# Layer 0's opening in a two-layer backbone: row blocks loaded first, LayerNorm applied on ACT, transposes per row block, and half of three column tiles computed early

## The chip, the cores and the metric

The kernel runs on one core of a Trainium2 chip. The metric is the device time of one launch in microseconds (us). The median of three runs of the kernel before is 1859.11 us.

## The reference, cut to what matters

A two-layer transformer-like backbone over 256 context tokens and 256 latent tokens, each of width 1024. At the start of a layer the tokens are normalised and modulated with vectors that come from a conditioning vector through a large matrix (adaLN); the result is projected by `w_in`, whose first columns feed the Hyena branch:

```python
s_lat, s_ctx = silu(c), silu(c_ctx)
mod   = s_lat @ ada_w[i] + ada_b[i]          # and mod_c from s_ctx
sh1, sc1, g1, sh2, sc2, g2 = split(mod, 6)
u  = layer_norm(h)  * (1 + sc1)  + sh1       # latent rows
uc = layer_norm(hc) * (1 + csc1) + csh1      # context rows
p_hy, p_sw, p_rw, p_df, p_gt = split(u @ w_in[i])
kf = rfft(filter made by a small MLP with sine activations)   # Hyena filter
y_hy = x2 * longconv(x1 * longconv(v, kf0), kf1)              # v, x1, x2: depthwise conv of p_hy
...                                          # three more branches, merge, output projection, FFN
```

## The kernel before, in words

**Tiling.** Tokens are held as four row blocks of 128 rows x 1024: `xn[0..3]` (two of context, two of latent tokens). After the norm they are transposed on TensorE into eight blocks of 128 channels x 512 tokens, one block for each k. A float32 product is done as three float32r matmuls: each operand is split into a rounded high part and a low remainder. `uh[k]`, `ul[k]` are the two parts of the modulated tokens; `whi`, `wlo` those of a 128x1024 weight tile, made by `wcut` (L193: ACT casts to `whi`, L197, then DVE or POOL subtracts into `wlo`, L201). One output column tile (128 output channels x 512 tokens) is `dense` (L243): for each of the eight k three matmuls of 512 columns into a PSUM bank, 24 in all. The first six column tiles of layer 0 are Hyena's (`hyena_cols`, L627); behind each a depthwise convolution (`conv3`, L321) of one ACT and two DVE instructions empties the bank.

**Modulation vectors.** `ada` (L362) computes them in groups of four 512 KB tiles of `ada_w`; each tile has two matmuls against a 32-column stationary tile. Then comes a tail: ACT copies the bank (L382), TensorE transposes it, DVE reduces it and adds the bias (L388, L390), and for scale groups adds one (L394). Group 0 is the shift for k = 0 to 3, group 2 the scale for k = 0 to 3, groups 1 and 3 the same for k = 4 to 7. `modulate` (L461) transposes two row blocks at a time and then, for each k, ACT makes `uh` (L475), POOL an intermediate (L476) and DVE `ul` (L478).

**Norm.** `stats` (L416) is two bn_stats, an aggregate and an add on DVE and a power on POOL; `norm` (L446) applies mean and scale, in the opening as one DVE instruction over 128x1024 (L451).

**Filter MLP.** `filter_mlp` (L497) loads four small tensors and does two steps, each one or two small matmuls, eight DVE instructions (L516, then `sin_rr`) and a Sin on ACT (L495). `filters` (L520) then makes each filter's spectrum: four matmuls with `fw3` (L531), DVE products, absolute values on ACT and sums on POOL for a norm `hyn` that the convolutions of column tiles 2 to 5 need, and eight products with the DFT matrix (L574).

**Order around the change.** `lockstep` (L279) writes instructions in a fixed order for PE, DVE, ACT and POOL: it draws from `start()` (L1786) and, by the credits that `start()` yields, from `ada`. Loads go on SP's queue in the order in which they are written; a load whose buffer is still in use waits, and all loads behind it wait too. In the opening `ada` takes its tiles from the buffers `w`, `whi`, `wlo` (seven in all, L375). Behind the fixed order `weave` (L267) mixes `hyena_cols` with `filters`, with a ratio of 0.7 that says how much filter work is written for each unit of dense work; there the framework's scheduler may move an instruction forward where it expects an engine to be free. `col_tile` (L257) also draws two steps of layer 0's remaining `ada` groups for each column tile (`N.rate`, `N.side`). PSUM has eight banks: three of tag `d`, four of tag `m`, one of tag `o`.

## Time and profile before

| | us |
|---|---|
| median of three runs | 1859.11 (1858.53 to 1861.16) |
| the profiled execution, whole | 1862.13 |
| its span from first to last instruction | 1860.1 |
| PE busy | 1702.9 (92%) |
| DVE busy | 1145.5 (62%) |
| ACT busy | 787.3 (42%) |
| POOL busy | 641.4 (34%) |
| span before the first Hyena column tile has been half computed | 55.35 |
| convolution of the sixth Hyena column tile starts | 107.41 |

A busy share of PE says that matmuls were in flight, not that they ran at the full clock; the views by stretch give the granted clock beside it. Idle time of an engine counts only where PE, which carries most of the chain that ended last, waits for it.

### The profile page before, as it was taken

The numbers are of one execution on the slowest core, as the hardware profiler recorded it, in microseconds if no ns is written. First come the engines' busy times: TensorE is split into PE (matmuls) and PEld (weight loads), VectorE is DVE, ScalarE is ACT, GpSimd is POOL, SyncE is SP. The second block draws the span as 40 slices with busy tenths as digits, with TensorE's granted clock in tenths as the row PEclk, the third lists the DMA queues.
The fourth block names the chain that finished last, engine by engine and source line by source line (L and its number), as shares of the span: only waits on it lengthen the run. The fifth ranks groups of instructions, "written<-read, shape, count | busy, mean of one in ns | idle before, by whom it ended". The sixth has DMA issues, their size and how long they took to land.

```text
span 1860.1 us, 36364 instructions
## 1 busy us (share of the span) xinstructions
PE 1702.9 (92%) x14618; PEld 1354.4 (73%) x14618; DVE 1145.5 (62%) x2204; ACT 787.3 (42%) x1579; POOL 641.4 (34%) x782
## 2 busy tenths in 40 slices
PE   6999999998999988999999998899788998879987
PEld 2566778776777766877787776677687887679964
DVE  5566456775665478544555657563765665758887
ACT  2323345653232346433334444334553343356632
POOL 2313144544544126101010164244454664131153
PEclk9999999999999999999999999999889999889999
DMA  8353321211111455344334556653123222646543
GB/s 302 126 198 113 130 69 57 83 57 45 45 56 55 148 196 189 120 150 139 125 102 138 180 175 210 198 179 130 47 88 97 88 65 82 237 142 189 184 145 113
DMA packets 73456, 241.37 MB, mean 130 GB/s; under 512 B 8518, under 2 KB 17096, under 8 KB 73032
## 3 DMA queue, kind: packets, MB, share of 16 engines
q1 hardware_dynamic: 69336, 229.80, 37.6%
q10 hardware_dynamic: 3952, 9.25, 1.5%
q8 instruction: 115, 1.88, 0.4%
q14 instruction: 53, 0.43, 0.1%
HBM read 235.84 MB, written 2.13 MB: 128 GB/s over the span
## 4 chain that ended last, share of the span: by engine, by line
PE 60%; DVE 15%; ACT 5%; DMA 4%; POOL 3%; issue 3%; POOLq 0%; SPq 0%; ACTq 0%; DVEq 0%
PE bkd L174 45%; PE bkm L174 8%; PE bkm L1362 2%; PE bko L174 2%; DVE wlo L201 2%; PE bkm L178 2%; ACT whi L197 2%; DMA w<-in_wdn 1%; DMA w<-in_wout 1%; DMA w<-in_win 1%; DVE sV L1340 1%; DVE dmx L978 1%; ACT dp L981 1%; POOL wlo L201 1%; DMA w<-in_adaw 1%
## 5 line engine op out<-in xcount | busy, mean ns | idle before, releaser
L174 PE MATMUL bkd<-uh,whi 128*128 128x256 f32 (+1 forms) x1624 | 585.7, 361 | 7.1 <-ACT whi L197 3.3
L174 PE MATMUL bkd<-uh,wlo 128*128 128x256 f32 (+1 forms) x1624 | 555.4, 342 | 3.5 <-DVE wlo L201 3.2
L174 PE MATMUL bkd<-ul,whi 128*128 128x256 f32 (+1 forms) x1624 | 552.9, 340 | 0.0
L197 ACT CAST whi<-w 128x256 fp32r<-128x256 f32 (+1 forms) x532 | 333.7, 661 | 268.4 <-PE bkd L174 116.6
L201 DVE TENSOR_TENSOR wlo<-w,whi 128x1024 fp32r<-128x1024 f32 (+3 forms) x247 | 284.2, 1155 | 195.7 <-ACT whi L197 194.8
L201 POOL TENSOR_TENSOR wlo<-w,whi 128x256 fp32r<-128x256 f32 (+2 forms) x328 | 276.9, 863 | 314.2 <-ACT whi L197 307.6
L174 PEld LDWEIGHTS bkd<-uh,whi 128*128 128x128 f32 x1624 | 311.8, 192 | 85.1 <-ACT whi L197 24.0
L174 PEld LDWEIGHTS bkd<-uh,wlo 128*128 128x128 f32 x1624 | 311.7, 192 | 40.8 <-DVE wlo L201 3.8
L174 PEld LDWEIGHTS bkd<-ul,whi 128*128 128x128 f32 x1624 | 312.9, 193 | 26.6 <-issue 0.7
L1722 POOL TENSOR_TENSOR fc<-fc,fc 128x256 f32<-128x256 f32 (+1 forms) x47 | 46.2, 982 | 331.3 <-DVE fc L329 312.0
L174 PE MATMUL bkd<-w,sst 128*32 128x512 f32 x348 | 81.0, 646 | 18.3 <-DMA w<-in_adaw 18.2
L1584 POOL TENSOR_TENSOR acc<-acc,tg 128x512 f32<-128x512 f32 (+1 forms) x32 | 32.5, 1017 | 145.4 <-DVE tg L1583 132.4
L324 ACT ACTIVATE fc<-bkd,vec 128x256 f32<-128x256 f32 (+1 forms) x94 | 60.8, 647 | 7.5 <-PE bkd L174 7.5
L327 DVE SCALAR_TENSOR_TENSOR fc<-bkd,vec,fc 128x255 f32<-128x255 f32 (+1 forms) x94 | 54.8, 583 | 11.5 <-ACT fc L324 11.5
L174 PE MATMUL bkd<-wlo,hh 128*128 128x512 f32 x126 | 52.4, 416 | 9.3 <-DVE wlo L201 6.2
L237 ACT CAST hh<-fc 128x256 fp32r<-128x256 f32 (+1 forms) x47 | 23.2, 493 | 84.9 <-POOL fc L1722 84.9
L329 DVE SCALAR_TENSOR_TENSOR fc<-bkd,vec,fc 128x255 f32<-128x255 f32 (+1 forms) x94 | 55.3, 589 | 2.9
L238 DVE TENSOR_TENSOR hl<-fc,hh 128x256 fp32r<-128x256 f32 (+1 forms) x47 | 25.6, 545 | 47.4 <-ACT hh L237 47.4
L174 PE MATMUL bkd<-y,wbh 128*128 128x512 f32 (+1 forms) x192 | 54.6, 369 | 0.0
L238 DVE TENSOR_TENSOR wbl<-wb,wbh 128x256 fp32r<-128x256 f32 x48 | 29.3, 611 | 37.0 <-ACT wbh L237 36.7
L174 PE MATMUL bkd<-whi,hh 128*128 128x512 f32 x126 | 48.5, 399 | 3.7 <-DVE fc L329 2.3
L981 ACT ACTIVATE dp<-bkm,dmx 128x512 f32<-128x512 f32 (+1 forms) x48 | 29.6, 617 | 48.2 <-DVE dmx L979 40.2
(474 smaller groups left out, 2995.6 us busy)
## 6 DMA issues: line engine op xcount, KB each, us to landing
w<-in_adaw SPq DMA_DIRECT2D x87, 512.0 KB, 3.9
w<-in_wup SPq DMA_DIRECT2D x82, 512.0 KB, 3.5
w<-in_wdn SPq DMA_DIRECT2D x66, 512.0 KB, 3.5
w<-in_wg SPq DMA_DIRECT2D x64, 512.0 KB, 3.5
w<-in_win SPq DMA_DIRECT2D x58, 512.0 KB, 3.6
w<-in_wout SPq DMA_DIRECT2D x24, 512.0 KB, 3.6
wb<-in_wbr SPq DMA_DIRECT2D x48, 128.0 KB, 3.4
pw<-in_wup SPq DMA_DIRECT2D x8, 512.0 KB, 4.5
```

Source lines behind the costliest of these rows:

```text
L174: self.nc.tensor.matmul(out, lhsT, rhs, start=start, stop=stop)
L178: self.nc.tensor.transpose(out, in_, self.ident[0:n, 0:n])
L197: self.nc.scalar.copy(hi[:, c], w[:, c])
L201: e.tensor_tensor(lo[:, c], w[:, c], hi[:, c].bitcast(F32), ALU.subtract)
L238: nc.vector.tensor_tensor(lo, src, hi.bitcast(F32), ALU.subtract)
L324: nc.scalar.activation(dst, ps, AF.Identity, bias=b, scale=w1)
L327: nc.vector.scalar_tensor_tensor(d3[:, :, 1:256], p3[:, :, 0:255], w0, d3[:, :, 1:256], ALU.mult, ALU.add)
L329: nc.vector.scalar_tensor_tensor(d3[:, :, 0:255], p3[:, :, 1:256], w2, d3[:, :, 0:255], ALU.mult, ALU.add)
L981: nc.scalar.activation(p[:, 0:n], ps[:, 0:n], AF.Exp, scale=scale, bias=mx[:, hc], accum_out=zz[:, hc])
L1362: nc.tensor.matmul(ps[r, o:o + 32], L(r, d, c, x, e, j), R[r, d, 2 * e + j, :], start=True, stop=True, tile_position=(r.start, r.start))
L1584: nc.gpsimd.tensor_tensor(acc, acc, tg[:, 0:n], ALU.add)
L1722: nc.gpsimd.tensor_tensor(ab[0], ab[0], ab[1], ALU.mult)
```

## The change

`start()` is written anew and `ada` is drawn by hand within it. The four row blocks are loaded first, with the small MLP tensors between them; the layer's `row` tensor moves from ACT's queue to SP's. The norm is applied on ACT. Transposes go by row block: `turned` takes four k of one row block as soon as that block is normalised, and holds all four `m` banks; `modulated` then works for each k on both halves of the tokens. `ada` gets nine buffers of its own and the bank of tag `o`; the MLP uses bank `d`. Three Hyena column tiles get the first half of their sum (k = 0 to 3) inside the fixed order (`begin`); the second half is taken up by `col_tile`. The first weight tile's low part is made on POOL. No filter step is in the opening any more, and the weave ratio is 1.5 in layer 0. Column tiles that were begun early do not draw steps of the remaining `ada` groups.

```diff
-    def dense(self, ps, hi, lo, c0, xh, xl, nk, t0, t1):
-        for k in range(nk):
+    def dense(self, ps, hi, lo, c0, xh, xl, nk, t0, t1, ks=None):
+        for k in ks or range(nk):
...
     def col_tile(self, src, part):
+        if self.begun:
+            rest_, ps = self.begun.pop(0)
+            yield from rest_
+            return ps
         hi, lo = self.wsplit(src)
...
-        nc.scalar.dma_start(self.row[l], a["row"][l].partition_broadcast(128))
+        (nc.scalar if l else nc.sync).dma_start(self.row[l], a["row"][l].partition_broadcast(128))
...
-            ps = self.bank("d")
+            ps = self.bank("o" if early else "d")
...
-                tag = ("w", "whi", "wlo", "w", "whi", "w", "wlo")[n % 7] if early else "w"
-                w = self.wp.tile([128, 1024], F32, tag=tag, name=tag, bufs=3 if tag == "w" else 2)
+                w = early.tile([128, 1024], F32, tag="ew", name="ew", bufs=9) if early else \
+                    self.wp.tile([128, 1024], F32, tag="w", name="w", bufs=3)
...
+    def turned(self, xn, ks):
+        at = {k: self.bank("m") for k in ks}
+        for i in range(4):
+            for k in ks:
+                self.tr(at[k][:, i * 128:i * 128 + 128], xn[i][:, k * 128:k * 128 + 128])
+            yield 0.1
+        self.at = at
+
+    def modulated(self, pool, l, ks):
+        for k in ks:
+            for s in range(2):
+                c = slice(s * 256, s * 256 + 256)
+                u = pool.tile([128, 256], F32, tag="u32", name="u32", bufs=3)
+                sc, sh, p = self.sc1p[l][:, 0, k, s:s + 1], self.mod[l][:, k, s:s + 1], self.at[k][:, c]
+                hi, lo = self.uh[k][:, c], self.ul[k][:, c]
+                nc.scalar.activation(hi, p, AF.Identity, scale=sc, bias=sh)
+                nc.gpsimd.tensor_scalar(u, hi.bitcast(F32), -1.0, sh, op0=ALU.mult, op1=ALU.add)
+                nc.vector.scalar_tensor_tensor(lo, p, sc, u, ALU.mult, ALU.add)
+            yield 0.2
...
+                                def norm(i):
+                                    nm = P()
+                                    m, rs = st[i]
+                                    nc.vector.tensor_scalar(nm, m, rs, -1.0, op0=ALU.mult, op1=ALU.mult)
+                                    nc.scalar.activation(xn[i], xn[i], AF.Identity, scale=rs, bias=nm)
...
+                                for i in range(4):
                                     nc.sync.dma_start(xn[i], a["xin"][i])
+                                    go(mlp, 1)
                                 N.vecs(0)
+                                tr = N.turned(xn, range(4))
+                                for i in range(4):
+                                    st[i] = N.stats(lp, xn[i])
+                                    if i:
+                                        norm(i - 1)
+                                        go(tr, 1)
+                                        go(ada, 1)
+                                norm(3)
+                                go(tr)
+                                go(ada, 1)
+                                load(0)
+                                go(mlp, 1)
+                                go(ada, 1)
+                                go(mlp, 1)
+                                go(ada, 2)
+                                cut(0, nc.gpsimd)
+                                go(ada, 2)
+                                load(1)
+                                load(2)
+                                go(ada, 1)
+                                go(N.modulated(lp, 0, range(2)))
+                                cut(1, nc.vector)
+                                go(N.modulated(lp, 0, range(2, 4)))
+                                cut(2, nc.vector)
+                                begin(0)
+                                go(ada, 2)
+                                begin(1)
+                                go(ada, 3)
+                                begin(2)
+                                go(ada, 4)
+                                tr = N.turned(xn, range(4, 8))
+                                go(tr)
+                                go(ada)
                                 nc.sync.dma_start(N.fw3, a["hw3"])
                                 nc.sync.dma_start(N.dft[:, 1024:1536], a["dft"][:, 1024:1536])
                                 nc.sync.dma_start(N.dft[:, 0:1024], a["dft"][:, 0:1024])
+                                go(N.modulated(lp, 0, range(4, 8)))
+                                yield 0.01
...
-                    N.weave(hyc, 0.7)
+                    N.weave(hyc, 0.7 if l else 1.5)
```

`go(g, n)` draws n steps from a generator: one step of `ada` is one 512 KB tile with its two matmuls, and each fifth step is a group's tail; one step of `mlp` in the first loop is one small load, later a whole MLP step.

## Rows read from the trace of the kernel before

**Rows 1.** Page: busy us of each engine, share of the span, instructions.
```profile
PE 1702.9 (92%) x14618; PEld 1354.4 (73%) x14618; DVE 1145.5 (62%) x2204; ACT 787.3 (42%) x1579; POOL 641.4 (34%) x782
```

**Rows 2.** Busy time by stretch (us, engines, PEclk granted, DMA share, GB/s).
```profile
0.00:55.35 55.35, 36.51 (x137) 14.94 (x138) 34.47 (x73) 16.78 (x28) 18.12 (x27) 0.88 0.77 284
55.35:107.40 52.05, 52.03 (x223) 32.33 (x225) 27.02 (x52) 15.49 (x21) 8.54 (x7) 1.00 0.47 165
...
8.00:10.00 2.00, 1.62 (x6) 0.40 (x8) 0.00 (x0) 0.00 (x0) 0.00 (x0) 1.00 1.03 418
...
28.00:30.00 2.00, 0.29 (x2) 0.29 (x3) 1.93 (x5) 0.89 (x2) 0.00 (x0) 0.50 1.02 406
...
52.00:54.00 2.00, 2.00 (x6) 1.55 (x6) 1.81 (x5) 0.74 (x2) 1.30 (x3) 0.50 0.52 133
```

**Rows 3.** Timeline of the load queues: start, us, queue, line, transfer.
```profile
0.72 0.41 ACTq L360 DMA_DIRECT2D row<-in_row  x1
0.72 0.38 SPq L341 DMA_DIRECT2D cc<-in_cc  x1
...
34.83 0.43 SPq L375 DMA_DIRECT2D whi<-in_adaw  x1
37.09 5.70 SPq L190 DMA_DIRECT2D w<-in_win  x2
```

**Rows 4.** DMA issues: size and median us from issue to landing.
```profile
w<-in_win SPq DMA_DIRECT2D x58, 512.0 KB, 3.6
```

**Rows 5.** Timeline of PE: `ada` tiles, transposes, dense matmuls, a filter matmul.
```profile
8.38 1.92 PE L174 MATMUL bkd<-w,sst 128*32 128x512 f32 x4 [8.38 <-DMA w<-in_adaw]
...
23.42 1.05 PE L174 MATMUL bkd<-whi,sst 128*32 128x512 f32 x4 [0.24 <-DMA whi<-in_adaw]
...
30.62 1.91 PE L178 MATMUL bkm<-cstt,x 128*128 128x128 f32 x8
...
53.61 0.63 PE L174 MATMUL bkd<-uh,whi 128*128 128x512 f32 x1
...
54.04 0.63 PE L174 MATMUL bkd<-ul,whi 128*128 128x512 f32 x1
...
67.42 0.39 PE L174 MATMUL bkd<-ul,whi 128*128 128x512 f32 x1
...
67.65 0.39 PE L174 MATMUL bkd<-uh,wlo 128*128 128x512 f32 x1
...
69.35 1.12 PE L174 MATMUL bkm<-fw,fhn 64*128 64x512 f32 x2
```

**Rows 6.** Timeline of DVE, ACT and POOL ahead of the first modulation, and its start.
```profile
12.67 0.54 DVE L516 TENSOR_SCALAR fx<-bkm,fvec 128x256 f32<-128x256 f32 x1 [8.66 <-PE bkm L174]
...
15.81 1.28 DVE L421 BATCH_NORM_STATS2 lnst<-x 128x6 f32<-128x512 f32 x2
15.93 0.42 ACT L495 ACTIVATE fh<-fx 128x256 f32<-128x256 f32 x1 [11.04 <-DVE fx L494]
...
18.19 0.81 DVE L451 TENSOR_SCALAR x<-x,lnmv,lnrs 128x1024 f32<-128x1024 f32 x1 [0.67 <-POOL lnrs L427]
...
29.09 0.57 ACT L382 COPY adas<-bkd 128x512 f32<-128x512 f32 x1
...
29.71 1.12 PE L178 MATMUL bkd<-cstt,adas 128*128 128x128 f32 x4 [5.23 <-ACT adas L382]
...
32.50 1.93 ACT L475 ACTIVATE uh<-bkm,mod,sc1p 128x256 fp32r<-128x256 f32 x4 [2.85 <-DVE sc1p L394]
...
33.68 1.86 DVE L478 SCALAR_TENSOR_TENSOR ul<-bkm,sc1p,u 128x256 fp32r<-128x256 f32 x4 [1.28 <-POOL u L476]
```

**Rows 7.** Timeline of the first weight tile's two parts, ACT and DVE.
```profile
45.54 1.05 ACT L197 CAST whi<-w 128x1024 fp32r<-128x1024 f32 x1
...
47.35 2.20 DVE L201 TENSOR_TENSOR wlo<-w,whi 128x1024 fp32r<-128x1024 f32 x1
```

**Rows 8.** Timeline of ACT: the convolution behind the sixth column tile starts.
```profile
107.41 0.78 ACT L324 ACTIVATE hx<-bkd,hyn 128x512 f32<-128x512 f32 x1 [3.66 <-PE bkd L174]
```

More of the change, by code (lines that the diff above doesn't have):

```diff
@@ L161, in __init__ @@
         self.lo = self.nc.vector
-        self.aside, self.done, self.feed = [], set(), None
+        self.aside, self.done, self.feed, self.begun = [], set(), None, []
         self.ps = ctx.enter_context(tc.tile_pool(name="ps", bufs=1, space=PSUM))
@@ L359, in rows, with ada @@
         self.row[l] = cp.tile([128, NROW], F32, tag="row", name="row", bufs=1)
-        nc.scalar.dma_start(self.row[l], a["row"][l].partition_broadcast(128))
-    def ada(self, l, groups, early=False):
+        (nc.scalar if l else nc.sync).dma_start(self.row[l], a["row"][l].partition_broadcast(128))
+    def ada(self, l, groups, early=None):
         nc, cp = self.nc, self.cp
@@ L382, in ada @@
             nc.scalar.copy(sb, ps)
-            p2 = self.bank("d")
+            p2 = self.bank("o" if early else "d")
             for c in range(4):
@@ L478, in modulate @@
             nc.vector.scalar_tensor_tensor(lo, p, sc, u, ALU.mult, ALU.add)
+    def turned(self, xn, ks):
[6 more added lines that the diff above has]
+    def modulated(self, pool, l, ks):
+        nc = self.nc
+        for k in ks:
[8 more added lines that the diff above has]
+            yield 0.2
     def sin_rr(self, pool, x, out):
@@ L504, in filter_mlp @@
             nc.sync.dma_start(t, a[nm])
-        yield 0.0
+            yield 0.0
         h1 = T([128, 256], "fh1")
         for step, dst in ((0, h1), (1, self.fhn)):
-            ps = self.bank("m")
+            ps = self.bank("d")
             if step == 0:
@@ L1779, in backbone @@
                         mlp = N.filter_mlp(fp)
-                        next(mlp)
                         fs = chain(N.filters(0, fp, spec), N.filters(1, fp, sp1))
@@ L1783, in backbone, with go, load, cut @@
                             xn = {i: lp.tile([128, 1024], F32, tag=f"x{i}", name="x") for i in range(4)}
-                            ada = N.ada(0, (0, 2, 1, 3), True)
+                            ada = N.ada(0, (0, 2, 1, 3), early=lp)
+                            P = lambda: lp.tile([128, 1], F32, tag="lnns", name="lnns", bufs=4)
+                            hl = [None, None, [lp.tile([128, 1024], F32R, name=f"w{y}") for y in "hl"]]
                             def start():
-                                def x(i):
+                                ws, st, cuts = [], {}, []
+                                def go(g, n=99):
+                                    for _ in range(n):
+                                        if next(g, None) is None:
+                                            break
+                                def norm(i):
[3 more added lines that the diff above has]
+                                    nc.scalar.activation(xn[i], xn[i], AF.Identity, scale=rs, bias=nm)
+                                def load(x):
+                                    ws.append(N.wload(a["win"][l, T_HY + x]))
+                                def cut(x, lo):
+                                    N.lo = lo
+                                    cuts.append(next(N.wcut(ws[x], 1, hl[x])))
+                                def begin(x):
+                                    ps = N.bank("d")
+                                    hi, lo = cuts[x]
+                                    part = lambda ks: N.dense(ps, hi, lo, lambda k: k * 128, N.uh, N.ul, 8, 0, 512, ks)
+                                    for _ in part(range(4)):
+                                        pass
+                                    N.begun.append((part(range(4, 8)), ps))
+                                for i in range(4):
@@ L1788, in x @@
                                     nc.sync.dma_start(xn[i], a["xin"][i])
-                                def norm(i):
-                                    N.norm(xn[i], xn[i], N.stats(lp, xn[i]))
-                                def modulate(i):
-                                    return N.modulate(lp, 0, 0, [xn[i], xn[i + 1]], i, range(4))
+                                    go(mlp, 1)
                                 N.vecs(0)
-                                yield -0.8
-                                x(0)
@@ L1811, in start @@
-                                norm(3)
                                 nc.sync.dma_start(N.dft[:, 1024:1536], a["dft"][:, 1024:1536])
-                                yield -0.5
                                 nc.sync.dma_start(N.dft[:, 0:1024], a["dft"][:, 0:1024])
-                                for i in (0, 2):
-                                    for _ in modulate(i):
-                                        pass
-                                    for _ in range(0):
-                                        next(fs, 0)
-                                    yield -0.8
@@ L1821, in start @@
-                                for x in range(4):
-                                    next(fs, 0)
-                                    if x % 2:
-                                        yield -0.4
+                                go(N.modulated(lp, 0, range(4, 8)))
+                                yield 0.01
                             N.u_tiles()
-                            N.lockstep(start(), ada, 1.0, True)
-                            N.pre = [N.wsplit(a["win"][l, T_HY + x]) for x in range(2)]
+                            N.lockstep(start(), iter(()), 1.0)
@@ L1828, in backbone @@
                             N.vecs(1)
-                            for i in (0, 2):
-                                N.weave(N.modulate(lp, 0, 0, [xn[i], xn[i + 1]], i, range(4, 8)), 0.0)
                     else:
```

12 lines of the change are left out of this document (removed).

## The prediction

> **What bounds the kernel now.** I read the busy times of the page first: PE has 1702.9 of 1860.1 us, DVE 1145.5 [rows 1]. So only time in which PE lacks work, or runs slowly, can be won. Then the opening by stretch. From 55.35 to 107.40 us PE is busy 52.03 of 52.05 us at granted clock 1.00; before that, 36.51 of 55.35 at 0.88 [rows 2]. The second stretch can only lose work; all that the change can win is in the first. Third, the load queue: group 3's last `ada` tile is issued at 34.83 and the weight tiles behind it at 37.09, where SP waits 5.70 us [rows 3], because seven shared buffers are full. Fourth, the clock: the granted clock is 0.50 at 28 to 30, with PE busy 0.29 of 2 us, and again at 52 to 54, after PE had waited [rows 2]. An `ada` tile takes 1.92 us at 8.38 and 1.05 us at 23.42; dense matmuls stand 0.43 us apart at 53.61 and 0.23 at 67.42 [rows 5]. These are the two levels, 1.2 and 2.4 GHz. At 8 to 10 the column reads 1.00 [rows 2], but the duration there is that of the lower level, and I go by the duration.
>
> **The measure of gain.** At 55.35 the kernel before has done all `ada` tiles, 30 of 32 transposes, 12 dense matmuls (half a column tile) and four filter matmuls, and needs 52.05 us more to the sixth convolution at 107.41 [rows 2, 8]. Call T3 the time at which the changed kernel has three column tiles done (72 matmuls). What it then lacks to the same point: 52.05, less 60 matmuls by 0.228 [rows 5] = 13.7, plus four filter matmuls by 1.05 (1.12 in flight, next start 1.05 later [rows 5]) = 4.2, less two transposes 0.25: 42.3. The four `ada` steps that begun tiles no longer draw are counted in this; they come later, in other column tiles. So the gain is 107.4 - 42.3 - T3 = 65.1 - T3: break-even is T3 = 65.1.
>
> **The change part by part.** *Loads.* Without `row` ahead and with the third place on SP's queue, the first row block is issued at about 0.72 + 2 x 0.43 = 1.6 and lands 3.6 later [rows 3, 4]: 5.2. Tiles then follow 1.25 us apart (half a megabyte at 418 GB/s [rows 2]); by 9.2 all four blocks are there, by 21 group 2's tiles, by 34 group 3's. Nine buffers remove the wait at 34.83. The price of `row` on SP is 0: it is queued behind all of this, and its first reader is stages away.
>
> *Norm.* Statistics cost DVE 1.7 a block (15.81 to 18.19 less the 0.67 waited for POOL [rows 6]). DVE's order puts block 1's statistics ahead of block 0's scale: 5.2 + 1.7 + 1.7 + 0.2 = 8.8. ACT's norm over 128x1024 I put at 1.2: a cast of that shape is 1.05 [rows 7]; 1.05 and 1.4 are the ends. Block 0 is ready at 10.0, block 3 at 15.0. On DVE the step took 0.81 [rows 6]. The Trainium skill (ScalarE: Activation LUTs, Rules for kernel authors) says to add and multiply on VectorE, not ScalarE; the rows agree, and by that rule block 0 would be ready 0.6 earlier.
>
> *First transposes and `ada` tiles.* PE's order alternates four transposes and one tile. At the lower clock a pair is 0.95 (half of 1.91) + 1.72 (an `ada` tile less the overlap of the next) [rows 5], so four pairs and the MLP's matmul (1.2) end at 22.0; at the higher clock they follow the norms and end at 17.4. I take 18.8: PE has no gap here such as it had in the trace, so the clock should rise midway.
>
> *To the first modulation.* Now DVE and ACT are serial, and PE's queue waits for them. MLP step one, 3.3 (12.67 to 15.93 [rows 6]), Sin 0.4: 22.5. Behind Sin in ACT's queue stands the tail of group 0 (copy 0.57, transposes 0.7 to 1.12 [rows 6]); behind that on PE the second MLP matmul, at 24.7, and group 2's four tiles. MLP step two and Sin: 28.5. The first weight's cast (1.05 [rows 7]): 29.55; copy: 30.1; transposes: 31.1; DVE's reduce and adds, 0.7 (an estimate: in the trace the tail's transposes end at 29.71 + 1.12 and modulation starts at 32.50, with a norm of 0.81 between, which leaves 0.86 [rows 6]): M = 31.8, against 32.50 before. With the two ends of the clock, 30.3 and 35.
>
> *First halves.* Modulated blocks come each 0.97 us (four ACT steps of 256 in 1.93), the first ready 1.18 + 2 x 0.47 = 2.1 after M [rows 6]. Two weight casts (1.05 each) stand between them on ACT, and one low part on DVE that took 2.20 while POOL worked [rows 7]. So the first half tile runs M + 2.1 to M + 7.7, paced by ACT. From there PE has work in order: two `ada` tiles 1.0, half tile 2.74, two tiles 1.0, a wait of 0.75 for the copy of group 1, its transposes 0.5, half tile 2.74, four tiles 1.9, sixteen transposes 1.8, tail 0.6, DVE 0.7: the second modulation starts at M + 21.5.
>
> *Second halves.* PE has nothing to do until M + 23.6, as all `m` banks are held, which shuts filters out. Then 36 matmuls take 8.3 at the higher clock, or 10.8 if the 2.8 us of idleness lower it, as at 52 to 54 [rows 2]. T3 = M + 31.9 to M + 34.4; I take 33.3.
>
> *Filters.* None stands ahead of the column tiles now, so two whole sets are woven in at 1.5. I price their matmuls as above and the denser weave at 0. Its ends: -2.8, if the scheduler moves filter matmuls into PE's gap, and +3, if PE queues behind the chain PE, DVE, ACT, POOL, PE. Small edits (bank `o` for `ada`, bank `d` for the MLP, the first low part on POOL) lie inside the waits above and cost 0; without that cover, 0.2 to 0.5 each.
>
> *Sum.* T3 = 31.8 + 33.3 = 65.1: gain 0. The loads' gain of some 9 us is spent on waits: DVE's two MLP steps now lie ahead of the modulation, and filter work that used to fill gaps is put behind. I add 1 us for filter matmuls that find a gap: 1861 for the profiled execution (1862.1, that is a span of 1860.1 and 2.0 around it), and 1858 against the median of 1859.1. A measurement can tell about 0.2%, 3.7 us; within that the forecast's own range is 1855.4 to 1862.8.
>
> **Rivals.** *The clock rises early and gaps are filled.* PE is steadily busy from 10 us on. M = 30.3 and no second drop: T3 = 62.2, gain 2.9; with filters in the 2.8 us gap 5.7: 1853.4. For it: dense work that was at 0.50 at 52 to 54 is at 1.00 from 55.35 on [rows 2]. Against: from 8.38 on it was busy over 6 us with `ada` tiles at the lower level [rows 2, 5]. The Trainium skill (TensorE: Matmul & The Clock Gate, Part 1) says that activity releases the throttle; by that rule this case holds, and the tiles at 8.38 do not agree with it.
>
> *The loads set the opening.* If the MLP's steps do not hold back group 2's tail, M follows its last tile (21) by 3: 24, T3 = 57.3, gain 7.8: 1851.3. The same queues on DVE and ACT speak against it. I give these two faster cases 0.36 together, as two independent mechanisms lead there.
>
> *Slower: PE stays at the lower clock through the first transposes.* Then the MLP's first matmul ends at 22.0 and everything that ACT and DVE do in series follows 3.2 us later: M = 35, T3 = 69.4 with the second drop, loss 4.3: 1863.4. It decides from M = 34.5 on, and each us of a densely woven filter chain adds to it. For it: the `ada` tiles at 8.38. Chance 0.22, in which I include 0.03 that the row blocks are not loaded first after all: then 4 us on the first block, the same 1863.
>
> **How the numbers follow.** No change that can be measured, 0.42, 1858.0. Faster 0.36, at 1851 to 1855. Slower 0.22, at 1863 and more. The range takes in the middle of both: from 1850.0, below the second faster case, to 1864.0, just past the slower one; some 0.1 is left out on either side.
>
> **What would show it.** In the changed trace: block 0 lands at about 5.2 and group 3's last `ada` tile by 34; the first modulated block starts at 31.8 (24 would be the loads' case, 35 the slower one); `ada` tiles turn from 1.9 to 1.05 us between 13 and 20; the second modulation starts at 53 with PE idle before it; the third convolution starts at 65 or a little later than three tiles' matmuls need. If the sixth convolution is reached by 100 or after 108, I am wrong, and the start of each modulation tells which step it was.

## The result: 1.6% slower

The changed kernel takes 1891.0 us (median) against 1860.1 us for the kernel before, on the same chip: ratio 1.0163, 95% interval 1.0136 to 1.0189. The profiled execution took 1889.9 us, with a span of 1887.7. Forecast were 1858.0 (1850 to 1864).

The page's engine line of the changed kernel; it answers [rows 1]:

```profile
PE 1714.5 (91%) x14618; PEld 1356.8 (72%) x14618; DVE 1140.3 (60%) x2203; ACT 792.1 (42%) x1583; POOL 637.2 (34%) x783
```

The same number of matmuls costs PE 11.6 us more, and the span is 27.6 longer. Where they went is in the windows of the changed kernel up to the convolution behind the sixth column tile (columns as in [rows 2]; PEclk stands ahead of the DMA share):

```profile
0.00:65.59 65.59, 38.01 (x154) 16.79 (x155) 22.89 (x61) 18.77 (x27) 9.60 (x18) 0.81 0.67 247
65.59:84.90 19.31, 19.31 (x32) 9.31 (x33) 9.55 (x15) 6.73 (x10) 7.57 (x11) 0.50 0.00 0
84.90:107.50 22.60, 19.02 (x70) 10.08 (x68) 14.72 (x24) 6.83 (x8) 9.72 (x7) 0.99 0.28 94
107.50:127.74 20.24, 20.24 (x85) 12.54 (x89) 8.97 (x22) 4.25 (x6) 0.00 (x0) 0.92 0.57 205
```

PE is busy 96.58 of these 127.74 us; before it was busy 88.54 of 107.40 [rows 2]. Of the 20.3 us by which the sixth convolution comes later, 12.3 are idleness and 8.0 are matmuls that run longer. Summed over the records, the column matmuls take 46.9 us against 37.4 and the filter's `fw,fhn` matmuls 12.0 against 8.0; shift/scale work is less by 4.3, since some of it comes later.

ACT's timeline of the changed kernel: the modulations and the sixth convolution, which answer [rows 6, 8].

```profile
34.76 0.56 ACT L502 ACTIVATE uh<-bkm,mod,sc1p 128x256 fp32r<-128x256 f32 x1 [2.20 <-DVE sc1p L398]
36.45 1.02 ACT L502 ACTIVATE uh<-bkm,mod,sc1p 128x256 fp32r<-128x256 f32 x2 [1.13 <-DVE ul L504]
38.60 0.56 ACT L502 ACTIVATE uh<-bkm,mod,sc1p 128x256 fp32r<-128x256 f32 x1 [1.13 <-DVE ul L504]
...
42.29 1.02 ACT L502 ACTIVATE uh<-bkm,mod,sc1p 128x256 fp32r<-128x256 f32 x2 [1.73 <-DVE ul L504]
...
63.21 0.56 ACT L502 ACTIVATE uh<-bkm,mod,sc1p 128x256 fp32r<-128x256 f32 x1 [2.36 <-DVE sc1p L398]
...
127.78 0.78 ACT L328 ACTIVATE hx<-bkd,hyn 128x512 f32<-128x512 f32 x1 [5.41 <-PE bkd L174]
```

Before, four `uh` steps ran one behind the other, 1.93 us for four [rows 6]. Now ACT waits 1.1 us or more, again and again, for DVE's `ul`: 36.45 to 38.60 is 2.15 us for one k.

PE's timeline of the changed kernel; it answers [rows 5]:

```profile
20.22 0.70 PE L174 MATMUL bkd<-fzt,fw 33*128 33x256 f32 x2
...
65.59 1.22 PE L174 MATMUL bkd<-uh,whi 128*128 128x512 f32 x2 [3.11 <-ACT uh L502]
...
68.02 2.07 PE L174 MATMUL bkm<-fw,fhn 64*128 64x512 f32 x2
...
70.61 0.63 PE L174 MATMUL bkd<-ul,whi 128*128 128x512 f32 x1
71.04 0.63 PE L174 MATMUL bkd<-uh,wlo 128*128 128x512 f32 x1
...
85.44 0.39 PE L174 MATMUL bkd<-ul,wh 128*128 128x512 f32 x1
...
107.46 1.05 PE L174 MATMUL bkm<-cstt,fab 128*128 128x1 f32 x8 [3.48 <-POOL fab L568]
```

Column matmuls stand 0.43 us apart at 70.61, and a pair of filter matmuls takes 2.07: the lower level of the clock, 1.2 GHz, from 65.59 to 84.9 without a pause in PE's work. From 103.98 to 107.46 PE waits 3.48 us for a filter sum (`fab`, the absolute values summed on POOL).

Last, the delay behind the kernel before (the same ACT or DVE instruction in both traces, median of the difference in start): 20.4 us at the sixth convolution, 27.5 at 300 us, 27.6 at the end. From the convolution to 300 us another 7.2 us are lost. Later stages move it by some 5 us in both directions, differently in each kernel, so I compare experiments at 300 us.

### The profile page after: what moved, and what is told of

It is laid out like the page before. It is cut to its first block, busy times and chain, and to the rows that moved or that the text cites. A ratio compares the mean times of both kernels' runs of the same rounds, so it can differ in the third digit from the quotient of the medians.

```text
span 1887.7 us, 36380 instructions
## 1 busy us (share of the span) xinstructions
PE 1714.5 (91%) x14618; PEld 1356.8 (72%) x14618; DVE 1140.3 (60%) x2203; ACT 792.1 (42%) x1583; POOL 637.2 (34%) x783
## 4 chain that ended last, share of the span: by engine, by line
PE 66%; DVE 16%; ACT 5%; DMA 5%; POOL 4%; issue 3%; SPq 0%; POOLq 0%; ACTq 0%; DVEq 0%
PE bkd L174 48%; PE bkm L174 10%; PE bko L174 3%; PE bkm L1389 2%; DVE wlo L201 2%; PE bkm L178 2%; ACT whi L197 2%; DMA w<-in_wdn 1%; DVE sV L1367 1%; DMA w<-in_win 1%; DVE dmx L1005 1%; ACT dp L1008 1%; DMA w<-in_wout 1%; POOL wlo L201 1%; DVE dp L1024 1%
## 5 line engine op out<-in xcount | busy, mean ns | idle before, releaser
L174 PE MATMUL bkd<-uh,whi 128*128 128x512 f32 (+1 forms) x1616 | 584.7, 362 | 18.2 <-ACT uh L502 8.3
L174 PE MATMUL bkd<-uh,wlo 128*128 128x512 f32 (+1 forms) x1616 | 555.0, 343 | 0.4 <-DVE wlo L201 0.2
L174 PE MATMUL bkd<-ul,whi 128*128 128x512 f32 (+1 forms) x1616 | 553.7, 343 | 1.2 <-DVE ul L504 1.2
L201 DVE TENSOR_TENSOR wlo<-w,whi 128x1024 fp32r<-128x1024 f32 (+3 forms) x245 | 275.6, 1130 | 197.4 <-ACT whi L197 196.8
L201 POOL TENSOR_TENSOR wlo<-w,whi 128x256 fp32r<-128x256 f32 (+3 forms) x329 | 278.2, 865 | 334.5 <-ACT whi L197 327.9
L1611 POOL TENSOR_TENSOR acc<-acc,tg 128x512 f32<-128x512 f32 (+1 forms) x32 | 32.5, 1017 | 143.1 <-DVE tg L1610 130.1
L174 PE MATMUL bkd<-w,sst 128*32 128x512 f32 x320 | 71.8, 638 | 7.8 <-DMA w<-in_adaw 7.8
L237 ACT CAST hh<-fc 128x256 fp32r<-128x256 f32 (+1 forms) x47 | 23.2, 493 | 84.9 <-POOL fc L1749 84.9
L238 DVE TENSOR_TENSOR hl<-fc,hh 128x256 fp32r<-128x256 f32 (+1 forms) x47 | 25.7, 546 | 47.3 <-ACT hh L237 47.3
L174 PE MATMUL bkd<-whi,hl 128*128 128x512 f32 x126 | 50.2, 400 | 0.0
```

The costliest lines, as they stand in the source:

```text
L174: self.nc.tensor.matmul(out, lhsT, rhs, start=start, stop=stop)
L201: e.tensor_tensor(lo[:, c], w[:, c], hi[:, c].bitcast(F32), ALU.subtract)
L237: nc.scalar.copy(hi, src)
L238: nc.vector.tensor_tensor(lo, src, hi.bitcast(F32), ALU.subtract)
L1611: nc.gpsimd.tensor_tensor(acc, acc, tg[:, 0:n], ALU.add)
```

## The experiments

Theories at the start: A, ACT and DVE take turns at the shared banks of `turned`; B, the filter work among the columns keeps the clock low and makes PE wait; C, the filter network's two steps (`mlp`) hold back the first modulation. Later O, the order of PE's queue; S, the side steps (remaining `ada` groups) that begun tiles no longer draw; D, F, P, T and Q are told in the texts that use them. The table has all runs; M1 and M2 are the starts of the modulations, "6th" that of the sixth convolution. Times are single executions but for the changed kernel, d4, e1 and f1, which are medians; the kernel before ran at 1860 to 1864 us beside them. M1, M2, 6th and delay are read from one execution each. Kernels whose code is the same up to the second modulation start it up to 1.5 us apart (48.6, 49.0 and 50.1 in d1, e3 and d4), so a difference of 1.5 us or less between two rows can't be told from nothing.

| kernel | M1 | M2 | 6th | delay at 300 | us |
|---|---|---|---|---|---|
| before | 32.5 | 47.4 | 107.4 | 0 | 1860.1 |
| changed | 34.8 | 63.2 | 127.8 | 27.5 | 1891.0 |
| a1_halves_apart | 34.6 | 58.8 | 121.5 | 20.9 | 1879.1 |
| a3_mlp_late | 26.6 | 59.3 | 125.4 | 27.0 | 1887.7 |
| a4_filters_late | 34.2 | 62.4 | 127.0 | 26.2 | 1889.0 |
| a5_apart_late | 34.0 | 57.7 | 117.7 | 16.2 | 1877.6 |
| c4_weave10 | 34.8 | 63.2 | 129.2 | 27.3 | 1892.1 |
| e4_order_alone | 33.9 | 53.3 | 119.3 | 18.8 | 1881.9 |
| c3_apart_filt | 34.9 | 65.6 | 116.9 | 19.3 | 1885.6 |
| c1_begin_late | 25.6 | 49.8 | 114.2 | 15.2 | 1872.1 |
| c2_begin_late_filt | 27.1 | 65.0 | 119.2 | 18.7 | 1882.7 |
| d1_mlp2_late | 25.4 | 48.6 | 111.9 | 14.6 | 1876.3 |
| d2_side | 25.2 | 50.7 | 122.2 | 13.7 | 1876.5 |
| d3_space | 25.9 | 50.6 | 113.9 | 13.9 | 1876.6 |
| e2_side_space | 25.8 | 51.1 | 115.9 | 8.0 | 1875.4 |
| e3_mlp_side | 25.5 | 49.0 | 117.1 | 7.7 | 1871.5 |
| d4_all | 26.0 | 50.1 | 112.2 | 2.6 | 1864.4 |
| e1_mlp_behind | 25.9 | 39.7 | 113.4 | 4.7 | 1867.4 |
| f1_mlp_last | 25.7 | 39.5 | 104.1 | -5.4 | 1859.0 |

**A, the shared bank.** The modulation's loops are swapped, so that ACT goes over the four banks of one token half before the next half:

```diff
-        for k in ks:
-            for s in range(2):
+        for s in range(2):
+            for k in ks:
...
-                                go(N.modulated(lp, 0, range(2)))
+                                md = N.modulated(lp, 0, range(4))
+                                go(md, 4)
                                 cut(1, nc.vector)
-                                go(N.modulated(lp, 0, range(2, 4)))
+                                go(md)
```

> The changed kernel with the two loops of the modulation exchanged: all four k of the context half first, then all four k of the latent half, so that ACT and DVE no longer read one PSUM bank in turn. Theory A (the shared bank): ACT's step for the second half of a k waits for DVE's step on the first half, 2.15 us a k in place of 0.97. Then the first half tile ends by 43.5 us (47.3 in the changed kernel), the second modulation begins by 59.5 (63.2), its last DVE step comes by 66 (78.4), and the sixth convolution (127.8) comes 8 us or more earlier; the time falls by about 8. Theory B (filter matmuls between dense ones hold PE at the lower clock from 65.6 to 84.9): only the 4 us ahead of the second modulation are won, PE is at the lower clock about as long as before, the sixth convolution comes 4 to 5 us earlier.

ACT's timeline of a1_halves_apart:

```profile
34.62 1.93 ACT L502 ACTIVATE uh<-bkm,mod,sc1p 128x256 fp32r<-128x256 f32 x4 [2.20 <-DVE sc1p L398]
...
58.79 3.75 ACT L502 ACTIVATE uh<-bkm,mod,sc1p 128x256 fp32r<-128x256 f32 x8 [2.36 <-DVE sc1p L398]
```

The same eight instructions now run in 3.75 us with no wait between them, and the second modulation, to its last `ul`, takes 4.9 us (58.8 to 63.7) instead of 15.2 (63.2 to 78.4). The turns at the bank are shown. They are not all of the 10.3 us: in a4 and e4, below, which keep the turns and have no filter products between the `ul` steps on DVE, the same stretch takes 10.0 us (62.4 to 72.4, 53.3 to 63.3). The turns cost some 5.1 of it, the filter products in DVE's queue the other 5.2. The half tile ends at 44.7, for the 43.5 expected, and the sixth convolution comes only 6.2 earlier, not 8: PE now waits for `fab` twice, 6.1 us together.

**B and C, each alone.** a3_mlp_late takes the network's steps from ahead of the first modulation to just ahead of `begin(0)` and `begin(1)`. a4_filters_late puts ten steps of the column work ahead of the filters, where the change has two, and then draws six filter steps at once. a5_apart_late is a1 and a4 together. c4_weave10 weaves at 1.0 where the change has 1.5.

> The changed kernel with the filter MLP's two steps moved behind the first modulation (one ahead of the first half tile, one ahead of the second). Theory C (the MLP's two serial steps on DVE and ACT hold up the modulation): the first modulation starts at 26 to 28 us in place of 34.8, and the second modulation and the sixth convolution come 5 to 7 us earlier. Rival: the wait only moves, as DVE's MLP steps now stand in PE's way behind the first modulation, or the loads hold: gain under 3 us at the sixth convolution. Theories A and B expect no more than that from this edit.

> The changed kernel with the filter steps written only after the second halves of the first two column tiles. Theory B: without filter matmuls among the first dense ones PE reaches the higher clock by 73 us (84.9 in the changed kernel), and the sixth convolution (127.8) comes 6 to 9 us earlier. Theory A: the second modulation is still paced by the shared bank, 2.15 us a k, and ends at 72; PE is sparse until then, the clock rises only behind it, and the sixth convolution comes 3 us earlier or less.

> Both edits, halves apart and filters late. Theories A and B together: the gains add, 12 to 17 us at the sixth convolution, and the time comes within 10 us of the kernel before. If A alone is the cause, no more than halves apart alone; if B alone, no more than filters late plus 4.

> The changed kernel with the filter work woven into the columns at a ratio of 1.0, not 1.5 (0.7 was the ratio of the kernel before). Theory D (the denser weave puts the filter's waits for DVE and POOL into PE's queue and keeps the clock low): the 3.5 us wait for fab is under 1, fewer than 35 of the 144 column matmuls run at the low clock (43), sixth convolution at 121 to 125 (127.78). Rival (the density does not matter, only where the filter work stands): within 1.5 us of 127.78.

C's first half holds: M1 comes at 26.6. But the sixth convolution gains only 2.4 and 300 us 0.5, as its rival had it: the second modulation still waits for PE. B alone fails in time, though its clock is there: it rises earlier (30 column matmuls at the lower level, not 43), but the filter steps, begun later, run closer together, and PE waits 8.6 us for `fab` (3.5 in the changed kernel). The density alone gives nothing that can be measured. A and B together give 10.1 at the sixth convolution, short of the 12 to 17 expected.

**O, the order of PE's queue.** In c1_begin_late (with A's edit, and the network's steps behind the first modulation) and e4_order_alone (alone, shown here), `begin` stands behind all shift/scale work:

```diff
-                                begin(0)
-                                go(ada, 2)
-                                begin(1)
-                                go(ada, 3)
-                                begin(2)
-                                go(ada, 4)
+                                go(ada, 9)
                                 tr = N.turned(xn, range(4, 8))
                                 go(tr)
                                 go(ada)
+                                for x in range(3):
+                                    begin(x)
```

> Base: the changed kernel with the two token halves of the modulation apart (as in the run with the halves apart) and the filter network's two steps behind the first modulation. Edit: the 36 matmuls of the three begun column tiles (k 0 to 3) are given to PE behind all the shift/scale matmuls and the second transposes, not among them. Theory O (PE takes its work in the order written; the begun matmuls, at the low clock and waiting for their modulated blocks, hold back the shift/scale matmuls and with them the second modulation): second modulation at 45 to 50 us (63.21 in the changed kernel, 58.79 with the halves apart), the 72nd column matmul ends by 68 and the sixth convolution starts at 106 to 112. Rival (the loads of the shift/scale weights or the clock set the second modulation): second modulation later than 54, sixth convolution later than 115.

> The changed kernel with one edit alone: the 36 matmuls of the begun tiles behind the shift/scale work and the second transposes. Halves, filter network and weave as in the changed kernel. Theory O (PE's order is worth most where the halves are not apart, since the begun matmuls wait for the first modulation, 10.2 us of half tile): second modulation 49 to 53 (63.21), delay at 300 us 15 to 20 (27.5). Rival (the shared banks set the second modulation's end whatever PE's order): last block of the second modulation later than 72, delay 23 or more.

ACT's and DVE's timelines of e4_order_alone, the start and the end of the second modulation:

```profile
53.29 0.56 ACT L502 ACTIVATE uh<-bkm,mod,sc1p 128x256 fp32r<-128x256 f32 x1 [2.35 <-DVE sc1p L398]
...
62.80 0.48 DVE L504 SCALAR_TENSOR_TENSOR ul<-bkm,sc1p,u 128x256 fp32r<-128x256 f32 x1 [1.22 <-POOL u L503]
```

PE's timeline of c1_begin_late:

```profile
36.74 1.12 PE L174 MATMUL bkd<-fh,fw 64*64 64x256 f32 x4 [7.43 <-ACT fh L522]
...
42.19 0.66 PE L178 MATMUL bko<-cstt,adas 128*128 128x128 f32 x4 [2.46 <-ACT adas L386]
...
48.78 0.48 PE L174 MATMUL bkd<-uh,whi 128*128 128x512 f32 x1
...
72.43 1.05 PE L174 MATMUL bkm<-cstt,fab 128*128 128x1 f32 x8 [2.61 <-POOL fab L568]
...
93.80 1.05 PE L174 MATMUL bkm<-cstt,fab 128*128 128x1 f32 x8 [3.48 <-POOL fab L568]
```

Theory O holds for the second modulation (49.8 and 53.3, from 63.2), and alone it is the largest single part, 8.8 us at 300. In c1 the column matmuls run at the higher level from the first (48.78, 0.48), and PE does not wait ahead of them. What is left is in the rows: 7.43 and 2.46 us for the network and a copy on ACT, 6.1 for `fab`. So c1's 72nd column matmul ends at 79.2, for O's 68, and its sixth convolution comes at 114.2, for 106 to 112.

**F, filter steps back in the opening.** c2 (on c1) and c3 (on a1) give the first four filter steps back to the opening, among the last shift/scale steps (`next(fs, 0)` and `go(ada, 1)` by turns), with their loads earlier.

> As the run before it, and the first four filter steps (four filter matmuls and the multiplications on DVE behind them) are given back to the opening, between the last shift/scale steps, with the loads of their two inputs ahead of the second and third column weights. Theory F (the filter work lay in waits of PE in the kernel before, and among the columns it lengthens them): sixth convolution 3 to 6 us earlier than in the run before it, second modulation at most 3 later. Rival (the columns hide the filter work, the opening does not): sixth convolution within 1 us or later.

> The changed kernel with the halves apart, begun tiles in their place, and the first four filter steps given back to the opening among the last shift/scale steps. Theory F: sixth convolution at 115 to 118 us (121.54 with the halves apart alone), second modulation 0 to 2 later than 58.79. Rival: sixth convolution at 120 or later.

In c2 F fails: the second modulation comes 15 us later. In c3 the sixth convolution is 4.6 earlier (116.9, in F's range), yet the second modulation is 6.9 later. The reason is in the windows of c2:

```profile
24.00:43.80 19.80, 8.41 (x39) 1.69 (x31) 12.42 (x29) 8.81 (x15) 5.83 (x9) 0.72 1.02 405
43.80:63.93 20.13, 20.13 (x48) 7.13 (x49) 4.91 (x9) 2.60 (x3) 6.62 (x5) 0.51 0.02 5
63.93:89.00 25.07, 25.07 (x98) 16.69 (x97) 14.70 (x30) 9.54 (x16) 5.26 (x10) 1.00 0.14 42
```

PE is busy for 20.13 us without a break at granted clock 0.51; four pairs of filter matmuls take some 8 us of them. Filter work fills gaps only if PE has gaps there; here, among shift/scale steps at the lower level, it lengthened the path.

**S, P and the rest of O.** Three edits on c1: the network's second step behind the shift/scale work (d1); begun tiles draw their side steps (d2); the filter sum is spaced from its absolute values (d3).

```diff
             rest_, ps = self.begun.pop(0)
+            for _ in range(self.rate):
+                next(self.side, None)
             yield from rest_
...
-        yield 1.0
+        yield 4.0
         nps = self.bank("m")
```

> Base: the kernel with the begun matmuls behind the shift/scale work (c1_begin_late: second modulation 49.75, sixth convolution 114.17, 1872.09 us). Edit: the second step of the filter network, whose matmul waited 7.4 us for its sine there with the shift/scale matmuls behind it on PE, is put behind all of them. Theory O (PE's order): second modulation at 42 to 45, sixth convolution 3 to 6 us earlier (108 to 111). Rival (the shift/scale weights land no earlier, or the wait turns up at the filter matmuls): second modulation later than 48, or sixth convolution less than 2 earlier.

> Base c1_begin_late. Edit: a begun column tile also draws the side steps (shift/scale work of a later stage) that a column tile draws, as in the kernel before; in the changed kernel four such steps moved to later columns. Theory S (these four steps and the 2.6 us for which PE waits near 158 us there make the delay grow from 6.8 us at the sixth convolution to 15.2 at 225): sixth convolution 2 to 3 us later, the delay from 250 us on 11 to 13.5, the time 2 to 4 us less than 1872. Rival (the four steps cost the same wherever they stand): the delay from 250 us on stays at 14.5 to 16.

> Base c1_begin_late. Edit: in the filter steps more column matmuls are put between the absolute values (ACT, then three additions on POOL) and the matmul that sums them (a pause of 4.0 in place of 1.0 in the weave's units, about 4 more groups of three matmuls at 1.5). Theory P (PE waits there, 2.6 and 3.5 us, because the matmul follows too close): both waits together under 2 us, sixth convolution 3 to 6 us earlier (108 to 111). Rival (POOL's additions come that late whatever is put between): waits stay above 4 us together, sixth convolution within 1.5 us of 114.17.

> The three edits above together on c1_begin_late. If theories O, S and P hold and add up: second modulation 42 to 45, sixth convolution at 104 to 110, time 1855 to 1864 us, level with the kernel before. If only one of them holds: 1866 to 1870.

> c1_begin_late with two of the three edits: the side steps drawn and the filter sum spaced, the network's second step in its old place. Delay behind the kernel before at 300 us: 15.2 with none, 13.7 with the side steps alone, 13.9 with the spacing alone, 2.6 with all three. Theory T (the side steps' matmuls fill the pause and keep PE at work, so that the waits for fab go and the clock stays up; the two belong together): delay 3 to 7. Rival (the network's second step is the one that is missing in each): delay 10 to 14.

> c1_begin_late with the other two: the side steps drawn and the network's second step behind the shift/scale work, the filter sum not spaced. Theory T: both waits for fab are there (4 to 6 us together), the clock falls behind them, delay at 300 us 10 to 14. Rival: delay 3 to 7.

Each alone gives 0.7 to 1.5 us at 300, no more than the scatter, and misses its theory: in d1 the wait moved to a copy on ACT behind the network's first sine, and M2 came only 1.2 earlier; in d3 the two waits for `fab` were still 4.6 us (2.6 and 2.0), as the rival had it. The whole times of d1, d2 and d3, 1876.3 to 1876.6, are even 4 us above c1's single execution; d2 was expected 2 to 4 below it. d2 shows S in an odd way: the sixth convolution is 8 us later, and after it the delay no longer grows. So it is in every kernel with that edit: from the sixth convolution to 300 us the delay goes from 14.8 to 13.7 (d2), 8.5 to 8.0 (e2), 9.7 to 7.7 (e3), 4.8 to 2.6 (d4); without it from 6.8 to 15.2 (c1), 4.5 to 14.6 (d1), 6.5 to 13.9 (d3), 20.4 to 27.5 (changed). Pair by pair (c1 and d2, d1 and e3, d3 and e2) the side steps are worth 9.5, 12.0 and 8.0 us after the columns. Part of that is waits that the kernels without the edit have; one of them in PE's timeline of the changed kernel:

```profile
170.02 1.06 PE L174 MATMUL bkd<-w,sst 128*32 128x512 f32 x8
173.73 0.57 PE L174 MATMUL bkd<-uh,whi 128*128 128x512 f32 x1 [2.64 <-DVE rn L1157]
```

In d2 the steps cost nearly as much among the columns: up to the sixth convolution PE is busy 7.2 us longer than in c1 (91.7 for 84.5). That holds their own matmuls and a lower clock behind the second wait for `fab` (0.68 in the window from 100 to 110; in c1 0.83 from 90 to 100, around the same wait); what each is worth was not taken apart. Either partner takes off some 6 us (e2 8.0, e3 7.7), both together 11 (d4). Theory T, that one pair belongs together, is not borne out: e2 lies just beyond its 3 to 7, and e3, which it put at 10 to 14, came out as e2, with both waits for `fab` still there (2.56 and 3.48). d4, all three edits together, missed its ranges: second modulation 50.1 (42 to 45), sixth convolution 112.2 (104 to 110), 1864.4 us (1855 to 1864).

**Q, ACT's queue.** In d4 the second sine of the network stands ahead of the second modulation on ACT, whose factors are there at 46.4 (the view ends at 51 us):

```profile
37.08 0.57 ACT L388 COPY adas<-bko 128x512 f32<-128x512 f32 x1
...
49.78 0.42 ACT L524 ACTIVATE fhn<-fx 128x256 f32<-128x256 f32 x1 [6.33 <-DVE fx L523]
50.10 1.46 ACT L504 ACTIVATE uh<-bkm,mod,sc1p 128x256 fp32r<-128x256 f32 x3
```

e1 puts the copy ahead of the first sine and the second step, its matmul now in bank `o`, into the middle of the second modulation; f1 puts that step behind the whole modulation (lines of f1 against the changed kernel):

```diff
-                                go(N.modulated(lp, 0, range(4, 8)))
+                                md = N.modulated(lp, 0, range(4, 8))
+                                go(md)
+                                go(mlp, 1)
```

> Base: d4_all (halves apart, begun matmuls behind the shift/scale work, side steps drawn, filter sum spaced; second modulation 50.10, delay behind the kernel before 2.6 us at 300). There ACT's copy of the third group of shift/scale sums stood 6.2 us behind the first sine of the filter network, and the second sine (49.78) stood 3.7 us in front of the second modulation, whose factors were there at 46.4. Edit: the copy goes ahead of the first sine, and the network's second step behind four of the eight second modulations (its matmul takes another bank). Theory Q (ACT's own order sets the second modulation in that kernel): second modulation at 41 to 46, sixth convolution at 105 to 109 (112.19), 1857 to 1862 us, 0 to 0.25% faster than the kernel before. Rival (the last shift/scale weights set it, or what is gained is lost at the filter matmuls that now come later): second modulation later than 47 or sixth convolution later than 111, and the time within 2 us of 1864.

> Base: e1_mlp_behind, where the second modulation began at 39.72 as theory Q has it, but its second half stood behind the second sine of the filter network (51.19) on ACT and behind that network's steps on DVE, and ended at 54.52. Edit: the network's second step behind all eight second modulations. Theory Q: last block of the second modulation at 45 to 47, the 72nd column matmul ends at 62 to 68 (71.98), sixth convolution at 104 to 109 (113.42), delay at 300 us between -5 and 0 (4.68), time 1857 to 1862. Rival (the filter matmuls, which need that step, now come so late that their waits for DVE and POOL fall among the last columns): last block as in Q, but sixth convolution later than 110 and delay at 300 us 2 or more.

ACT's timeline of e1_mlp_behind:

```profile
39.72 1.93 ACT L504 ACTIVATE uh<-bkm,mod,sc1p 128x256 fp32r<-128x256 f32 x4 [1.89 <-DVE sc1p L400]
51.19 0.42 ACT L524 ACTIVATE fhn<-fx 128x256 f32<-128x256 f32 x1 [9.54 <-DVE fx L523]
51.51 1.91 ACT L504 ACTIVATE uh<-bkm,mod,sc1p 128x256 fp32r<-128x256 f32 x4
```

and of f1_mlp_last, with its windows:

```profile
39.54 3.75 ACT L504 ACTIVATE uh<-bkm,mod,sc1p 128x256 fp32r<-128x256 f32 x8 [1.89 <-DVE sc1p L400]
...
51.37 0.41 ACT L524 ACTIVATE fhn<-fx 128x256 f32<-128x256 f32 x1
```

```profile
0.00:38.56 38.56, 22.54 (x114) 8.34 (x115) 17.72 (x49) 16.85 (x23) 9.07 (x17) 1.00 0.96 367
38.56:66.04 27.48, 26.23 (x112) 16.28 (x111) 17.55 (x36) 9.15 (x15) 11.15 (x13) 1.00 0.43 152
66.04:104.12 38.08, 35.72 (x141) 19.74 (x139) 21.03 (x40) 10.48 (x14) 8.21 (x5) 1.00 0.43 141
```

One step in the wrong place on one queue held half a modulation for 9.5 us (e1). So e1 has the early second modulation, but not the rest of what Q said: its sixth convolution came at 113.4 (105 to 109) and its time at 1867.4 (1857 to 1862). With the step behind the modulation (f1), the modulation ends at 44.5, the 72nd column matmul at 66.0, and PE is idle for 104.12 - 84.49 = 19.6 us up to the sixth convolution, as in the kernel before (18.9), and the granted clock does not fall from 15.5 us on. (Ahead of that the column reads 1.00 too, but an `ada` tile at 12.47 took 1.92 us, the lower level.) Q holds in f1; the delay at 300 us, -5.4, is a little better than the -5 to 0 expected. It flatters f1: its traced execution took 1853.9 us, one of the fastest of its twelve (1853.5 to 1864.8), and that of the kernel before 1862.1, where the medians are 1859.0 and 1860.0. By the medians, too, the whole loss is undone, with the changed loads, norms and begun tiles still in the kernel. In time f1 is the kernel before: 1859.0 against 1860.0, ratio 0.9994 (0.9979 to 1.0008). d4 is at 1.0016 (1.0002 to 1.0030), e1 at 1.0021 (1.0005 to 1.0036). None beats it.

## Why the prediction was wrong

**The loads** were right: the first statistics run at 5.26, where 5.2 was said for the block. **M** came at 34.76, for 31.8, inside its ends of 30.3 and 35. The network's first matmul ended at 20.9, for 18.8: the clock rose at 17, as the prediction allowed (13 to 20), but two of the four tiles ahead ran at the lower level (1.92 and 1.85), and PE had waited 1.18 us ahead of the first. The second sine ended at 31.1, for 28.5; and the tail, put at 0.7, took 1.45, since one small addition on DVE ran 0.98 us.

**T3** was put at 65.1; the 72nd column matmul ended at 92.86. The 27.8 us lie, by the prediction's own steps: M 3.0; *first halves* (M + 7.7, measured M + 12.6) 4.9; from there to the second modulation (13.8, measured 15.8) 2.0; *second halves* (11.8, measured 29.7) 17.9. So the largest error is in what follows the second modulation: by the rate of 0.97 us its last block would be ready 5.0 us behind its start (2.1 and three times 0.97), and it took 15.2; and PE's matmuls from 65.59 to 84.9, filters among them, ran at the lower level. Of the 17.9, some 7.4 come back after T3, because filter work that I had counted behind T3 stood ahead of it: 127.8 - 92.9 is 34.9, for 42.3.

**The step that failed first** is "Modulated blocks come each 0.97 us". The row behind it is right [rows 6], but it belongs to a loop over four banks. The new function's loop takes both halves of one bank in turn, as the diff shows, and ACT then waits for DVE: 2.15 us for a k. The Trainium skill has the rule (PSUM — Partial Sum Buffer, section PSUM bank collisions raise a hardware error): the compiler's scheduler makes instructions of two engines that touch one bank, in the same quadrant of partitions, depend on each other, two readers too. The trace agrees, with the 1.13 us waits and with a1, where they are gone. I had taken a rate of one loop order for a property of the operation. Alone it is worth 6.6 us at 300.

**The second** is in "PE has work in order", where I let 36 begun matmuls stand among the shift/scale steps that feed the second modulation and gave that order no price. The sum put the second modulation at 53.3, where the kernel before had it at 47.4, so 5.9 us of lateness were even in it, but not as an edit with a price; e4 measured 8.8 at 300 for it.

**The third** is the filter weave "priced at 0", with ends of -2.8 and +3. Its cost was neither of the two mechanisms alone: the stretch from 65.59 runs at 1.2 GHz, where the 36 matmuls were given 8.3 or 10.8, and one wait of 3.48 came at 104. The kernel before has no wait for a filter sum up to its sixth convolution. "All `m` banks are held, which shuts filters out" was wrong too: DVE's timeline of the changed kernel has the filter's `ft` ahead of the last `ul`, so the modulation waited for filter matmuls, some 5.2 us as worked out under A.

```profile
70.13 0.69 DVE L559 TENSOR_TENSOR ft<-bkm,dft 128x512 f32<-128x512 f32 x1 [0.82 <-PE bkm L174]
...
77.29 0.69 DVE L559 TENSOR_TENSOR ft<-bkm,dft 128x512 f32<-128x512 f32 x1 [2.03 <-PE bkm L174]
77.90 0.47 DVE L504 SCALAR_TENSOR_TENSOR ul<-bkm,sc1p,u 128x256 fp32r<-128x256 f32 x1
```

Moving the filters alone (a4), or thinning them (c4), gave 1.4 and 0.2 us, no more than the scatter; what they cost depends on what else waits.

**The fourth** is "they come later, in other column tiles" for the side steps, with no price. They cost 8 to 12 us after the sixth convolution, where I had assumed that nothing changes. Drawn among the columns again they cost 2.0 to 8.0 there, so that giving them back was worth 1.5, 5.9 and 6.8 us at 300 in the three pairs.

The rivals pointed to M and the first clock only. The slower one, with M at 35, would have given 1863: M was there, and it was a tenth of the loss. That the parts are no sum is part of the answer: edits worth 0.5 to 8.8 us alone on the changed kernel, and 0.7 to 1.5 alone on c1, undo 33 together, because each alone only brings up the next wait. Which share of the 8 to 12 us behind the columns is idleness and which is the side work itself was only reckoned, not tried: from the sixth convolution to the same point (300 us in the kernel before) PE is idle 12.6 us in c1 and 8.0 in d2, and busy 188.4 and 183.5. Nor did a run undo the norms on ACT or the order of the loads.

## What to carry to other kernels

A duration read from a row holds for that loop order; when a change reorders accesses of two engines to one accumulator bank, ask first who takes turns with whom. For each engine, list the queue ahead of every instruction that the path needs: work that only waits goes behind work that feeds it, on PE, on ACT and on DVE alike. And work that filled gaps, such as filter or side steps, has a price wherever it is moved to; find the gap that takes it up before calling it free.

## What the runs showed of the hardware

PE can be busy without a pause at the lower level of the clock: from 65.59 to 84.90 in the changed kernel it was busy 19.31 of 19.31 us at granted clock 0.50, after a wait of 3.1 us, and in c2 20.13 of 20.13 at 0.51. In both, 64-row filter matmuls (2.07 a pair) stood between the others; in the changed kernel the clock rose at 85.2, behind column matmuls alone. a4 comes nearest to a test: there the same column matmuls start at the lower level after the same wait of 3.1 us, without filter matmuls between them, and the clock rose at 70.5, 5.7 us after the first of them (19.6 in the changed kernel). That is one execution of each. With the same filter matmuls in c1, in a stretch that began at the higher level, it did not fall: PE was busy 21.02 of 21.02 us from 48.78 on at 1.00. The Trainium skill (TensorE: Matmul & The Clock Gate, Part 1) says that activity releases the throttle; the two stretches at 0.5 show that a busy PE was not enough here.

A DVE addition of 128x8 took 0.98 us at 33.53 in the changed kernel and 0.17 at 55.75; in the first case POOL was writing a weight's low part at the time (32.15, 2.34 us), and the addition ended 0.02 us after it. So it was in a1 and e4 (0.98 and 0.99 us, ending with POOL's step). That POOL is the cause was not tried. If it is, the first low part on POOL, which the prediction put at 0, cost M some 0.8 us.

```profile
32.15 2.34 POOL L201 TENSOR_TENSOR wlo<-w,whi 128x1024 fp32r<-128x1024 f32 x1 [18.85 <-ACT whi L197]
...
33.53 0.98 DVE L394 TENSOR_TENSOR mod<-mod,vec 128x8 f32<-128x8 f32 x1
```
